# A hybrid decoder block in one program: a new priority rule for the instruction order, and one projection moved forward

## The chip, the cores and the metric

The kernel runs on one core of a Trainium2 chip. The metric is device time in microseconds, from the first to the last instruction of one launch; lower is better. The time of the kernel before is the median of 3 runs.

## The reference

Everything is float32. `x` is 512 tokens by 1024 channels. It is normalised (RMS over the channels, times a gain) and multiplied by one weight matrix `w_in` of 1024 by 6936. The product is cut into pieces that feed two mixers:

- **Mixer A**, sparse attention: 8 query heads of 64 in 2 groups. Each head attends to compressed keys (31 blocks of 32 tokens, through a small two-layer network with weights `cmp_w1`, `cmp_w2`), to selected keys (with 8 blocks and the best 16 wanted, all causal keys) and to a window of 512 (again all causal keys). Three softmaxes, each times a sigmoid gate, are summed; the sum is times silu(`z_n`), then times `w_nsa_o`, which gives `y_a`.
- **Mixer B**, retention: 4 heads, keys of 128, values of 256, in 4 chunks of 128 tokens. Each chunk adds the decayed product inside the chunk and a product with a state carried from chunk to chunk. The output is normalised per head, times silu(`z_r`), then times `w_ret_o`, which gives `y_b`.

The result is `x + rmsnorm((sigmoid(m_a) * y_a + sigmoid(m_b) * y_b) @ w_out)`. `z_n`, `z_r`, `m_a`, `m_b`, `q_r`, `k_r`, `v_r` are all columns of `h @ w_in`.

## The kernel before

**Arithmetic.** Every operand of a large product is split into a high and a low part (`whi`, `wlo` for weights, `hTh`, `hTl` for the activations), and a product is three matmuls: high by high, high by low, low by high. ScalarE (ACT) makes most of the high parts by a copy, VectorE (DVE) most of the low parts by a subtraction; GpSimd (POOL) makes some.

**Blocks.** The large projections are blocks of 512 columns. A block is 4 loads of 512 KB into a ring of 4 buffers (`raw`), 8 splits of 128 rows into a ring of 9 pairs (`whi`, `wlo`), and 4 tiles of 24 matmuls. A tile accumulates in one of two PSUM banks (`ACC`). Its tail, a coroutine, empties the bank with DVE or ACT and so frees it for the next tile but one.

**Order of the blocks.** `main()` (L1231 on) issues: the attention projections, the two products of the compression (`hidden`, L643), `z_n` (called Z here), then for each of two head pairs hp the blocks ZR (`z_r`), QK (`q_r`, `k_r`) and VR (`v_r`); then for each half of the output columns MA (`m_a`), MB (`m_b`), the product with `w_nsa_o` and that with `w_ret_o`; last `w_out`. MA0 is the first half of `m_a`, and so on. The attention of mixer A runs beside these blocks, as coroutines of their own.

**How the order of instructions is made.** Every engine works through its own instructions in the order in which the program gives them. A planner (`class Order`, L36 to L99) makes this order while the program is built: it keeps a model time `now` of TensorE (PE) and a model time at which each other engine will be free. Every piece of work is a coroutine with a fixed priority (smaller first) that yields the model time of its next input. `run()` takes the first coroutine, by priority, whose input is at least `LAG` (150 ns) old. A coroutine that has its input is issued even if its engine has much work queued before it. The splits of weights are issued as soon as the ring has room (`splitter` priority 1, `split_lo` priority 0, L358 to L391); attention has priorities 1 to 3, the blocks of `main()` 9: TensorE runs them where nothing else is ready.

**Waits that the change touches.** `tail_zr` (L920) keeps silu(`z_r`) in `zt[t]`, one set for both head pairs; so its copy for pair 1 waits until retention chunk t of pair 0 is finished (flag `ret0t`). `tail_qk` (L943) frees its bank with four DVE instructions at L198. `tail_m` (L1099) multiplies by the row of norms (`rsrow`, L185), then takes the Sigmoid on ACT; for MA0 it waits for flags of the retention or of the attention, since its buffers `sgs` lie on theirs. `ga_split` (L1116) waits until all of retention is finished, and then splits mixer A's output for the product with `w_nsa_o`, with POOL. `ret` (L980) is the retention of one chunk, in which chunk t waits for the state of chunk t - 1, and chunk 0 of pair 1 for the end of pair 0.

Of the kernel before, what the change touches and what calls it, by code (L numbers as in the profile page):

```python
# [27 lines left out]
NR, NW = 4, 9  # L28
MAIN = 9
LAG, PE_LAG = 150.0, 110.0  # L30
MARGIN = 50.0
WAKE = 10
# [3 lines left out]
class Order:  # L36
# [3 lines left out]

    def __init__(self):
        self.now = 0.0
        self.eng = {"act": 0.0, "dve": 0.0, "pool": 0.0, "dma": 0.0}
        self.ring = 500.0
        self.port = 0.0
        self.cos = []
        self.flags = set()

    def spawn(self, gen, prio):
        self.cos.append([prio, len(self.cos), 0.0, gen])  # L50
        self.cos.sort(key=lambda c: c[:2])
# [4 lines left out]
    def pe(self, cost, r=0.0):  # L56
        self.now = max(self.now, r + LAG + PE_LAG) + cost
        return self.now + 47
# [4 lines left out]
    def op(self, e, cost, r=0.0, port=False):  # L63

        self.eng[e] = self.begin(e, r, port) + cost
# [10 lines left out]
    def run(self):  # L76
        while self.cos:
            best = None
            for c in self.cos:
                w = c[2]  # L80
# [4 lines left out]
                w += LAG + (MARGIN if c[0] < MAIN else 0.0)  # L85
# [6 lines left out]
            if not callable(best[2]):  # L92
# [27 lines left out]
def block_kernel(ctx: ExitStack, tc, x, xT, g_pre, w_in, b_gate, pe_k, w1_k, w2_k,  # L120
# [51 lines left out]
    def act(o, i, func=AF.Copy, r=0.0, **kw):  # L172
        S.activation(o, i, func, **kw)  # L173
        return od.op("act", act_ns(o, i, lazy(*kw.values())), r)
# [90 lines left out]
    zt = [at(30 + 2 * t, 512) for t in range(NT)]  # L265
# [4 lines left out]
    sgs = [at(o, 512) for o in (28, 30, 8, 10, 12, 14, 16, 18)]  # L270
# [53 lines left out]
    add_block(w_in, C_Z, 512, KD, True)  # L324
    for hp in range(2):
        add_block(w_in, C_ZR + hp * 512, 512, KD)
        add_qk(hp)
        add_block(w_in, C_VR + hp * 512, 512, KD)
    for half in range(2):
        add_block(w_in, C_MA + half * 512, 512, KD)  # L330
        add_block(w_in, C_MB + half * 512, 512, KD)
        add_nsa_o(half)
        add_block(w_ret_o, half * 512, 512, KD)
# [23 lines left out]

    def splitter():  # L358
        for i, (_, n, _, perm) in enumerate(loads):
            for k in range(2):  # L360
# [3 lines left out]
                while len(raws) <= i:  # L364
                    load_next()
                r = max(raws[i][1], done[-1] if done and not own else 0.0)
                yield r
# [25 lines left out]
    used = [0]  # L393

    class Block:
# [10 lines left out]
        def ready(self, kt):  # L406
            i = self.base + kt
            return parts[i][2] + PE_LAG if i < len(parts) else (lambda: i < len(parts))
# [51 lines left out]
    def h_split():  # L460
        for k in range(KD):
            yield lambda: xTr[k] > 0
            yield xTr[k]
# [4 lines left out]
    def h_low(k, e):  # L468
        yield e
# [3 lines left out]
    def norms():  # L473

        for t in range(NT):
            yield lambda: t in xr_
            yield xr_[t]
            e = act(xt[t], xt[t], AF.Square, scale=1.0 / 32.0, accum_out=ss[:, t:t + 1], r=xr_[t])
        yield e
        e = ts(ss, ss, 1e-6, None, OP.add, r=e)  # L480
        e = tt(rs3[:, 0, :], ss, nhalf, OP.pow, e, "pool")
        yield e
# [7 lines left out]
        yield e  # L490
# [23 lines left out]
    def rope16(v, t, shape, r, e="dve"):  # L514
# [15 lines left out]
        tt(t2[hi], v[lo], bc(ropen[:, t, 24:32]), OP.mult, r, e)  # L530
        return tt(v[al], t1, t2, OP.add, 0.0, e)
# [8 lines left out]
    def keysT(kd, off, br, t, r):  # L540
# [4 lines left out]
        yield e  # L545
# [3 lines left out]
        yield e  # L549
# [4 lines left out]
    def vals(src, br, t, r):  # L554
        for g in range(2):
            sv = src[:, g * 64:(g + 1) * 64]
            e = act(VS[:, t, br, g, g, :], sv, r=r)
            e = sub_split(VS[:, t, br, g, 1 - g, :], sv, VS[:, t, br, g, g, :], e, "pool")
        return e

    def tail_a(t, ps, e, ring):
        yield od.need("const", "rs")
        kn = yield from NAT.get()
        yield max(e, constr["rope"], rsr[0])
        e = act(kn, ps, r=e, scale=rs(t))
        ring.put(ps, e)
        yield e
# [13 lines left out]
        yield ep  # L581
# [12 lines left out]
    def tail_c(t, ps, e):  # L594
        kn = yield from NAT.get()
        yield e
        e = act(kn[:, 0:280], ps[:, 0:280], r=e, scale=rs(t))
        ACC.put(ps, e)
        yield e
# [10 lines left out]
    def tail_z(j, ps, e):  # L610
        yield od.need("rsrow")
        th = yield from NAT.get()
        yield max(e, rwr[0])
        e = tt(szn[:, j, :], ps, rsrow, OP.mult, e)
        ACC.put(ps, e)
        yield e
        e = act(th, szn[:, j, :], AF.Tanh, r=e, scale=0.5)
        yield e
# [4 lines left out]
    def gates():  # L623
        yield od.need("C0", "C1", "C2", "C3")
        e = act(gate, gate, AF.Tanh, scale=0.5)
        yield e
# [3 lines left out]
    def x_split(i):  # L630
# [4 lines left out]
        yield e  # L635
# [25 lines left out]
    def compress(i, ph, e):  # L661
        yield e
# [9 lines left out]
        yield e  # L672
        pv = pt[:, 0:256].rearrange("p (k s c) -> p k s c", k=2, s=2)
        e = act(u, pv[:, :, 0, :], r=e)
        yield e
        e = tt(hx, pv[:, :, 1, :], u, OP.add, e)
        PT.put(pt, e)
        tt(u, hx, hx, OP.mult)
        ts(u, u, 0.044715, 1.0, OP.mult, OP.add)
        e = tt(u, u, hx, OP.mult)  # L680
        yield e
        e = act(u, u, AF.Tanh, scale=0.7978845608028654, r=e)
        yield e
        e = stt(hx, u, 1.0, hx, OP.add, OP.mult, e)
        po = yield from PT.get()
        if i == 0:
# [3 lines left out]
            yield e  # L690
            pv = po[:, 0:64].rearrange("p (g c) -> p g c", g=2)
            e = act(kc[:, :, 0, :], pv, scale=-0.5, r=e)
            yield e
            e = stt(kc[:, :, 1, :], pv, -0.5, f(kc[:, :, 0, :]), OP.mult, OP.subtract, e)
        else:
# [9 lines left out]
            yield e  # L705
# [11 lines left out]
    def tail_q(t, ps, e):  # L717
        qn = yield from NAT.get()
        yield e
        e = act(qn, ps, r=e, scale=rs(t, 1))  # L720
        ACC.put(ps, e)
        yield e
# [4 lines left out]
        yield e  # L727
        e = sub_split(qs[:, :, 1, :], qv, qs[:, :, 0, :], e)
        NAT.put(qn, e)
        for g in range(2):  # L730
# [5 lines left out]
            yield ep  # L736
# [17 lines left out]
    def att_cmp(t):  # L754
# [7 lines left out]
        yield e  # L762
# [6 lines left out]
        od.op("dve", 350)  # L769
        ts(mx, mx, -1.0e38, None, OP.max)  # L770
# [626 lines left out]
```

## Time and profile before

| | us |
|---|---|
| median of 3 runs (lowest to highest) | 555.47 (554.83 to 558.17) |
| the profiled execution's own time | 556.03 |
| its span in the profile | 554.2 |
| TensorE busy | 527.7 |
| VectorE busy | 385.9 |
| ScalarE busy | 257.4 |
| GpSimd busy | 69.7 |

The span is the time from the first to the last instruction in the trace. Busy times are of the whole span, and the kernel has stages with different limits. Matmuls overlap, and their ends are modelled; so the busy time of TensorE says where it had nothing to do, but not that it worked at its peak elsewhere.

### The profile page before, as it was taken

How to read it: one execution, taken by the hardware profiler on the slowest of the kernel's cores; microseconds unless marked ns; L12 is line 12 of the kernel's file. 1: busy time of each engine (PE TensorE's matmuls, PEld its weight loads, DVE VectorE, ACT ScalarE, POOL GpSimd, SP SyncE). 2: the span in 40 equal slices, each digit the busy share in tenths (PEclk: the TensorE clock that was granted, in tenths of full speed). 3: DMA queues.
4: the chain of work that ended last, by engine and by line, in shares of the span. 5: the costliest groups of instructions: out<-in, count | busy, mean ns of one | idle time of the engine just before them, and what ended most of it. 6: DMA issues, size and time to landing. Idle time of an engine off the chain costs nothing.

```text
span 554.2 us, 7494 instructions
## 1 busy us (share of the span) xinstructions
PE 527.7 (95%) x2642; PEld 441.0 (80%) x2642; DVE 385.9 (70%) x871; ACT 257.4 (46%) x550; POOL 69.7 (13%) x92
## 2 busy tenths in 40 slices
PE   8989996999999996999987999999999999999995
PEld 7778785888778785888876888887888888888885
DVE  6589899979989999877785658774545253526443
ACT  5572685647558466555371445442424143304411
POOL 1021102000100112212221233022000000000000
PEclk9989998999999999899999999999999999999998
DMA  8881037401301402305031231327422251414022
GB/s 294 290 246 41 20 97 200 160 2 38 115 0 39 135 20 84 107 2 170 1 116 56 81 109 38 115 56 247 152 77 69 84 152 30 157 43 152 1 76 114
DMA packets 34837, 55.22 MB, mean 100 GB/s; under 512 B 4336, under 2 KB 14448, under 8 KB 34800
## 3 DMA queue, kind: packets, MB, share of 16 engines
q1 hardware_dynamic: 34800, 54.75, 31.7%
q8 instruction: 20, 0.33, 0.2%
q14 instruction: 17, 0.14, 0.1%
HBM read 52.64 MB, written 2.10 MB: 99 GB/s over the span
## 4 chain that ended last, share of the span: by engine, by line
PE 68%; DVE 21%; DMA 4%; issue 3%; ACT 2%; SPq 1%; POOL 0%; DVEq 0%; POOLq 0%; ACTq 0%
PE bank L206 63%; DVE wlo L185 5%; PE bank L210 5%; DVE arena_f L194 3%; DVE arena_r L185 3%; DVE arena_f L816 3%; DVE arena_f L185 2%; DMA raw<-in_w_in_dram 2%; DMA arena_f<-in_x_dram 2%; DMA arena_f<-in_xT_dram 1%; DVE arena_f L198 1%; DVE nat L198 1%; ACT arena_f L173 1%; SPq L452 1%; ACT arena_r L173 1%
## 5 line engine op out<-in xcount | busy, mean ns | idle before, releaser
L173 ACT ACTIVATE whi<-raw 128x512 fp32r<-128x512 f32 x148 | 89.4, 626 | 60.1 <-PE bank L206 45.8
L185 DVE TENSOR_TENSOR wlo<-raw,whi 128x512 fp32r<-128x512 f32 x150 | 105.7, 745 | 7.2 <-ACT whi L173 6.5
L206 PE MATMUL bank<-whi,hTh 128*128 128x512 f32 x256 | 100.8, 409 | 6.3 <-DVE nat L198 4.8
L206 PE MATMUL bank<-wlo,hTh 128*128 128x512 f32 x256 | 96.8, 393 | 0.4 <-DVE wlo L185 0.4
L206 PE MATMUL bank<-whi,hTl 128*128 128x512 f32 x256 | 96.9, 394 | 0.0
L206 PE MATMUL bank<-arena_r 128*128 128x256 f32 (+2 forms) x328 | 73.0, 342 | 1.7 <-DVE arena_r L185 1.6
L173 ACT ACTIVATE arena_r<-bank 128x512 fp32r<-128x512 f32 (+2 forms) x80 | 45.0, 570 | 55.8 <-PE bank L210 53.3
L206 PE MATMUL bank<-hTh,whi 128*128 128x512 f32 x160 | 63.5, 397 | 0.1
L206 PE MATMUL bank<-hTh,wlo 128*128 128x512 f32 x160 | 62.6, 391 | 0.0
L206 PE MATMUL bank<-hTl,whi 128*128 128x512 f32 x160 | 62.3, 390 | 0.0
L206 PEld LDWEIGHTS bank<-whi,hTh 128*128 128x128 f32 x256 | 48.4, 189 | 14.9 <-DVE nat L198 5.3
L185 DVE TENSOR_TENSOR arena_r<-bank,arena_r 128x512 fp32r<-128x512 f32 (+2 forms) x72 | 46.6, 656 | 18.4 <-ACT arena_r L173 18.1
L206 PE MATMUL bank<-arena_r,whi 128*128 128x512 f32 x192 | 59.1, 389 | 0.0
L206 PEld LDWEIGHTS bank<-arena_r 128*128 128x128 f32 x328 | 51.1, 192 | 9.9 <-DVE arena_r L185 3.3
L206 PEld LDWEIGHTS bank<-whi,hTl 128*128 128x128 f32 x256 | 48.2, 189 | 10.8
L206 PEld LDWEIGHTS bank<-wlo,hTh 128*128 128x128 f32 x256 | 48.5, 190 | 8.7 <-DVE wlo L185 0.8
L206 PE MATMUL bank<-whi,arena_r 128*128 128x512 f32 (+1 forms) x176 | 49.0, 353 | 0.0
L210 PE MATMUL bank<-ident,arena_f 128*128 128x128 f32 (+2 forms) x262 | 40.9, 279 | 6.2 <-DVE arena_f L185 3.4
L210 PEld LDWEIGHTS bank<-ident,arena_f 128*128 128x128 f32 (+2 forms) x262 | 32.2, 142 | 17.0 <-DVE arena_f L185 5.6
L206 PEld LDWEIGHTS bank<-arena_r,whi 128*128 128x128 f32 x192 | 36.0, 188 | 7.5
L173 ACT ACTIVATE arena_f<-arena_f,stat 128x512 f32<-128x512 f32 (+3 forms) x64 | 35.3, 554 | 12.0 <-DVE stat L816 12.0
L206 PE MATMUL bank<-wlo,arena_r 128*128 128x512 f32 (+1 forms) x104 | 35.3, 349 | 4.7 <-DVE wlo L185 4.7
(118 smaller groups left out, 726.4 us busy)
## 6 DMA issues: line engine op xcount, KB each, us to landing
raw<-in_w_in_dram SPq DMA_DIRECT2D x43, 512.0 KB, 4.4
raw<-in_w_in_dram SPq DMA_DIRECT2D x18, 256.0 KB, 3.1
arena_f<-in_x_dram SPq DMA_DIRECT2D x8, 512.0 KB, 6.9
raw<-in_w_ret_o_dram SPq DMA_DIRECT2D x8, 512.0 KB, 4.7
raw<-in_w_out_dram SPq DMA_DIRECT2D x8, 512.0 KB, 5.0
arena_f<-in_xT_dram SPq DMA_DIRECT2D x8, 256.0 KB, 6.2
raw<-in_cmp_w_k_dram SPq DMA_DIRECT2D x8, 256.0 KB, 4.5
arena_f<-in_rope_r_dram SPq DMA_DIRECT2D x8, 256.0 KB, 2.6
```

Source lines behind the costliest of these rows:

```text
L173: S.activation(o, i, func, **kw)
L185: (V if e == "dve" else G).tensor_tensor(o, a, b, op=op)
L194: V.tensor_scalar(o, a, s1, s2, op0=op0, op1=op1)
L198: V.scalar_tensor_tensor(o, a, s, b, op0=op0, op1=op1)
L206: T.matmul(ps, a, b, start=start, stop=stop)
L210: T.transpose(ps, a, idn)
L452: DMA.dma_start(xTf[k], xT[k * P:(k + 1) * P, :])
L816: V.tensor_tensor_reduce(pv[:, b, :], sv[:, b, :], maskp[:, 512 - L:512], 1.0, -NEG, OP.add, OP.min, nm[:, b:b + 1])
```

## The change

`PLAN` gives the order of the blocks, in which MA0 stands between Z and the first ZR. A coroutine can now name the engine that its next instruction needs (`yield e, "dve"`); it is then held back while that engine has more than `SLACK` (700 ns) of work queued by the model. Priorities may be functions: a weight split has priority 0 if its part is at most `SOON` (2) parts ahead of what `main()` is at, and 4 otherwise. The model's costs change: 8 ns more for every operation, inputs of dependent operations on one engine counted, read-outs of accumulators counted. `either` lets the model choose DVE or POOL where POOL was fixed. `zt` has a set for each head pair: pair 1's lies on buffers of the attention, so its tail waits for the attention's end (`ATT`) and no longer for `ret0t`. `sgs[0]` to `sgs[3]` get memory of their own, `sgs[4]` to `sgs[7]` lie on pair 0's `zt`.

```diff
+PLAN = (("Z", 0), ("MA", 0), ("ZR", 0), ("QK", 0), ("VR", 0), ("ZR", 1), ("QK", 1), ("VR", 1),
+        ("MB", 0), ("NO", 0), ("RO", 0), ("MA", 1), ("MB", 1), ("NO", 1), ("RO", 1))
+SOON = 2
+ISSUE = 8.0
+SLACK = 700.0
...
     def op(self, e, cost, r=0.0, port=False):
-        self.eng[e] = self.begin(e, r, port) + cost
+        self.eng[e] = self.begin(e, r, port) + cost + ISSUE
...
-            for c in self.cos:
-                w = c[2]
+            for c in sorted(self.cos, key=lambda c: (c[0]() if callable(c[0]) else c[0], c[1])):
+                w, e = c[2] if isinstance(c[2], tuple) else (c[2], None)
...
-                w += LAG + (MARGIN if c[0] < MAIN else 0.0)
+                w += LAG + (0.0 if c[0] == MAIN else MARGIN)
+                if e:
+                    w = max(w, self.eng[e] - SLACK)
...
+    def either(n, r):
+        return "dve" if od.begin("dve", r, True) + 1.04 * n <= od.begin("pool", r, True) + 2.36 * n else "pool"
...
-    zt = [at(30 + 2 * t, 512) for t in range(NT)]
+    zt = [[at((8 if hp else 30) + 2 * t, 512) for t in range(NT)] for hp in range(2)]
-    sgs = [at(o, 512) for o in (28, 30, 8, 10, 12, 14, 16, 18)]
+    sgs = [bp.tile([P, 512], FT, name=f"sg{i}") for i in range(4)] + [at(o, 512) for o in (30, 32, 34, 36)]
...
-                od.spawn(split_lo(p, hi, lo, src, vh, vl, e), 0)
+                od.spawn(split_lo(p, hi, lo, src, vh, vl, e), rank(p))
+                nxt[0] = p + 1
...
     def split_lo(p, hi, lo, src, vh, vl, r):
+        yield lambda: rank(p)() == 0 or od.eng["dve"] <= od.now + SLACK
         yield r
-        c = size(vl)
-        e = "dve" if od.begin("dve", r, True) + 1.04 * c < od.begin("pool", r, True) + 2.36 * c else "pool"
-        r = sub_split(vl, src, vh, r, e)
+        r = sub_split(vl, src, vh, r, either(size(vl), r))
...
+    def rank(p):
+        return lambda: 0 if p <= wanted[0] + SOON else 4
...
     def tail_zr(hp, t, ps, e):
-        yield od.need("C0", "C1", "C2", "C3", "cmp0", "cmp1", *([f"ret{hp - 1}{t}"] if hp else []))
-        yield e
-        e = act(zt[t], ps, r=e, scale=rs(t, 2))
+        yield od.need("C0", "C1", "C2", "C3", "cmp0", "cmp1", *(ATT if hp else ()))
+        yield e, "act"
+        e = act(zt[hp][t], ps, r=e, scale=rs(t, 2))
...
     def tail_m(half, i, ps, e):
-        if half == 0 and i >= 2:
-            yield od.need(*(RETA if i >= 6 else ATT))
-        elif half == 0:
-            yield od.need("qk13", "ret10")
+        if half == 0 and i >= 4:
+            yield od.need(f"ret0{i - 4}")
...
-            gar[0] = sub_split(gal[:, j, :], szn[:, j, :], gah[:, j, :], e, "pool")
+            gar[0] = sub_split(gal[:, j, :], szn[:, j, :], gah[:, j, :], e, either(512, e))
...
-    od.spawn(splitter(), 1)
+    od.spawn(splitter(), lambda: rank(nxt[0])())
```

Besides these, some 60 lines of the form `yield e` become `yield e, "act"`, `"dve"` or `"pool"`.

## Rows read from the trace of the kernel before

**Rows 1.** Page, part 1: busy us, share of span, instructions.

```profile
PE 527.7 (95%) x2642; PEld 441.0 (80%) x2642; DVE 385.9 (70%) x871; ACT 257.4 (46%) x550; POOL 69.7 (13%) x92
```

**Rows 2.** Busy time by stretch: length, then engines, granted clock, DMA share, GB/s.

```profile
0.00:40.00 40.00, 35.66 (x171) 30.39 (x172) 27.02 (x66) 23.77 (x47) 6.01 (x23) 0.96 0.86 277
...
80.00:95.00 15.00, 10.32 (x73) 9.43 (x72) 14.79 (x32) 9.13 (x19) 3.98 (x3) 0.96 0.77 209
95.00:216.00 121.00, 119.02 (x626) 98.31 (x626) 111.69 (x301) 75.21 (x177) 11.24 (x10) 0.99 0.21 66
216.00:222.00 6.00, 1.25 (x7) 1.00 (x6) 6.00 (x9) 2.17 (x10) 2.33 (x3) 0.84 0.40 119
222.00:227.00 5.00, 5.00 (x17) 4.02 (x17) 4.67 (x22) 2.13 (x9) 0.67 (x1) 0.51 0.67 229
...
280.00:301.00 21.00, 16.17 (x83) 12.87 (x83) 16.70 (x37) 9.23 (x17) 5.37 (x6) 1.00 0.33 100
...
379.00:544.00 165.00, 164.90 (x734) 136.74 (x734) 73.01 (x115) 50.56 (x90) 1.32 (x3) 1.00 0.32 102
544.00:554.20 10.20, 4.42 (x37) 4.21 (x36) 4.35 (x10) 0.95 (x4) 0.86 (x2) 0.85 0.27 103
```

**Rows 3.** Timeline near 216 us: start, duration, engine, line, tiles, count [idle before].

```profile
216.61 4.16 DVE L185 TENSOR_TENSOR wlo<-raw,whi 128x512 fp32r<-128x512 f32 x5
...
220.70 0.86 DVE L198 SCALAR_TENSOR_TENSOR nat<-bank,rs,arena_f 128x256 f32<-128x256 f32 x2
...
221.62 0.80 PE L206 MATMUL bank<-whi,hTh 128*128 128x512 f32 x1 [4.75 <-DVE nat L198]
```

**Rows 4.** Waits, 280 to 301 us: us in total, times, longest.

```profile
PE bank L210 <- DVE arena_f L185: 3.4, 2, 2.7
...
PE bank L206 <- ACT arena_f L173: 1.3, 1, 1.3
```

**Rows 5.** Timeline near 297 us.

```profile
296.20 0.70 POOL L185 TENSOR_TENSOR rv<-rv,nhalf 128x2 f32<-128x2 f32 x1 [11.07 <-DVE rv L192]
...
297.84 0.87 DVE L198 SCALAR_TENSOR_TENSOR nat<-bank,rs,arena_f 128x256 f32<-128x256 f32 x2
```

**Rows 6.** Waits, 76 to 97 us.

```profile
PE bank L206 <- DVE wlo L185: 4.7, 2, 2.8
```

**Rows 7.** Groups by line and form, whole span: busy us, mean ns, idle before.

```profile
L185 DVE TENSOR_TENSOR wlo<-raw,whi 128x512 fp32r<-128x512 f32 x150 | 105.7, 745 | 7.2 <-ACT whi L173 6.5 <-PE bank L210 0.4
L185 DVE TENSOR_TENSOR arena_f<-bank,rsrow 128x512 f32<-128x512 f32 x20 | 13.7, 687 | 32.3 <-PE bank L206 32.1
L198 DVE SCALAR_TENSOR_TENSOR nat<-bank,rs,arena_f 128x256 f32<-128x256 f32 x32 | 13.7, 475 | 2.4 <-PE bank L206 2.1 <-DMA arena_f<-in_rope_r_dram 0.2
...
L173 ACT ACTIVATE arena_f<-arena_f 128x512 f32<-128x512 f32 x16 | 10.0, 628 | 30.8 <-DVE arena_f L185 30.5
```

**Rows 8.** Timeline of ACT: both table loads of the span, and what follows them.

```profile
0.72 1.28 ACT L1317 ACT_TABLE_LOAD   x1 [0.72 <-PEq L1376]
2.02 0.20 ACT L1317 ACTIVATE ss<-nhalf 128x1 f32<-128x1 f32 x1
...
350.01 1.28 ACT L173 ACT_TABLE_LOAD   x1
355.50 0.63 ACT L173 ACTIVATE arena_f<-arena_f 128x512 f32<-128x512 f32 x1 [4.21 <-DVE arena_f L185]
```

**Rows 9.** Timeline: retention's matmuls, pair 1's first chunk, weight splits, the split after retention.

```profile
278.42 2.41 PE L206 MATMUL bank<-arena_r 128*128 128x256 f32 x18
...
324.41 0.75 DVE L198 SCALAR_TENSOR_TENSOR arena_r<-bank,rs,arena_r 128x512 fp32r<-128x512 f32 x1 [2.54 <-ACT arena_r L173]
...
345.06 3.09 DVE L185 TENSOR_TENSOR wlo<-raw,whi 128x512 fp32r<-128x512 f32 x5
...
371.01 7.49 DVE L185 TENSOR_TENSOR wlo<-raw,whi 128x512 fp32r<-128x512 f32 x5
...
371.11 6.83 POOL L185 TENSOR_TENSOR arena_r<-arena_f,arena_r 128x512 fp32r<-128x512 f32 x4 [5.45 <-ACT arena_r L173]
```

More of the change, by code (lines that the diff above doesn't have):

```diff
@@ L57, in pe @@
         self.now = max(self.now, r + LAG + PE_LAG) + cost
-        return self.now + 47
+        return self.now + 75
     def begin(self, e, r=0.0, port=False):
@@ L91, in run @@
             assert best is not None, f"nothing can be issued {[c[3].__name__ for c in self.cos]} {sorted(self.flags)}"
-            if not callable(best[2]):
+            if isinstance(best[2], tuple):
+                self.now = max(self.now, best[2][0] + LAG, self.eng[best[2][1]] - SLACK)
+            elif not callable(best[2]):
                 self.now = max(self.now, best[2] + LAG)
@@ L323, in block_kernel @@
     add_w1(w1_v)
[L324 to L333, printed above, removed]
+    for name, i in PLAN:
+        if name == "Z":
+            add_block(w_in, C_Z, 512, KD, True)
+        elif name == "QK":
+            add_qk(i)
+        elif name == "NO":
+            add_nsa_o(i)
+        elif name == "RO":
+            add_block(w_ret_o, i * 512, 512, KD)
+        else:
+            add_block(w_in, {"ZR": C_ZR, "VR": C_VR, "MA": C_MA, "MB": C_MB}[name] + i * 512, 512, KD)
     for half in range(2):
@@ L364, in splitter @@
                 while len(raws) <= i:
-                    load_next()
+                    yield lambda: len(raws) > i or len(raws) < NR or len(parts) > 2 * (len(raws) - NR) + 1
+                    if len(raws) <= i:
+                        load_next()
                 r = max(raws[i][1], done[-1] if done and not own else 0.0)
-                yield r
+                yield r, "act"
                 m = n // 2
@@ L391, in split_lo @@
             load_next()
-    used = [0]
+    used, wanted = [0], [0]
+    def rank(p):
+        return lambda: 0 if p <= wanted[0] + SOON else 4
     class Block:
@@ L407, in ready @@
             i = self.base + kt
+            wanted[0] = max(wanted[0], i)
             return parts[i][2] + PE_LAG if i < len(parts) else (lambda: i < len(parts))
@@ L897, in att_sum @@
         low = yield from NAT.get()
-        yield a["e"]
+        yield a["e"], "act"
         e = act(low[m], po[o], r=a["e"])
-        yield e
+        yield e, "dve"
         e = tt(low[m], po[m], low[m], OP.add, e)
         PO.put(po, e)
-        yield e
+        yield e, "pool"
         gv = szn[m, :, t * P:(t + 1) * P]
-        e = tt(gv, low[m].rearrange("p (j c) -> p j c", j=4), gv, OP.mult, e, "pool")
+        e = tt(gv, low[m].rearrange("p (j c) -> p j c", j=4), gv, OP.mult, e, either(512, e))
         NAT.put(low, e)
@@ L997, in ret @@
             ek = act(knh, kf[t])
-            yield ek
-            ek = sub_split(knl, kf[t], knh, ek, "pool")
+            yield ek, "pool"
+            ek = sub_split(knl, kf[t], knh, ek, either(256, ek))
         pa = yield from PS.get()
@@ L1265, in main @@
             yield from hidden(i)
-        blk = Block(8, 512)
-        for j in range(4):
-            ps, e = yield from tra(blk, j, j == 3, *hT_of)
-            od.spawn(tail_z(j, ps, e), 1)
-        for hp in range(2):
+        for name, i in PLAN:
+            if name in ("NO", "RO"):
+                blk = Block(4 if name == "NO" else 8, 512)
+                xh, xl = (gah, gal) if name == "NO" else (gbh, gbl)
+                if name == "NO":
+                    yield od.need("ga")
+                yield (gar if name == "NO" else gbr)[0] + PE_LAG
+                for ft in range(4):
+                    ps, e = yield from tra(blk, ft, ft == 3, lambda kt: xh[:, kt, :], lambda kt: xl[:, kt, :])
+                    od.spawn((tail_ya if name == "NO" else tail_yb)(i, ft, ps, e), 1)
+                continue
@@ L1271, in main @@
             blk = Block(8, 512)
             for t in range(NT):
-                ps, e = yield from nat(blk, t, 512, t == NT - 1)
-                od.spawn(tail_zr(hp, t, ps, e), 1)
-            blk = Block(8, 512)
-            for t in range(NT):
-                ps, e = yield from nat(blk, t, 512, t == NT - 1)
-                od.spawn(tail_qk(hp, t, ps, e), 1)
-            blk = Block(8, 512)
-            for t in range(NT):
-                ps, e = yield from nat(blk, t, 512, t == NT - 1)
-                od.spawn(ret(hp, t, ps, e), 1)
@@ L1283, in main @@
-        od.spawn(ga_split(), 1)
-        for half in range(2):
-            for i in range(2):
-                blk = Block(8, 512)
-                for ft in range(4):
-                    ps, e = yield from tra(blk, ft, ft == 3, *hT_of)
-                    od.spawn(tail_m(half, i * 4 + ft, ps, e), 1)
-            blk = Block(4, 512)
-            yield od.need("ga")
-            yield gar[0] + PE_LAG
-            for ft in range(4):
-                ps, e = yield from tra(blk, ft, ft == 3, lambda kt: gah[:, kt, :], lambda kt: gal[:, kt, :])
-                od.spawn(tail_ya(half, ft, ps, e), 1)
-            blk = Block(8, 512)
-            yield gbr[0] + PE_LAG
-            for ft in range(4):
-                ps, e = yield from tra(blk, ft, ft == 3, lambda kt: gbh[:, kt, :], lambda kt: gbl[:, kt, :])
-                od.spawn(tail_yb(half, ft, ps, e), 1)
+                if name in ("Z", "MA", "MB"):
+                    ps, e = yield from tra(blk, t, t == 3, *hT_of)
+                    od.spawn(tail_z(t, ps, e) if name == "Z" else tail_m(i, t + 4 * (name == "MB"), ps, e), 1)
+                else:
+                    ps, e = yield from nat(blk, t, 512, t == NT - 1)
+                    od.spawn({"ZR": tail_zr, "QK": tail_qk, "VR": ret}[name](i, t, ps, e), 1)
@@ L1302, in merged @@
+            if (name, i) == ("VR", 1):
+                od.spawn(ga_split(), 1)
         def merged(kt):
```

201 lines of the change are left out of this document (102 added, 99 removed).

## The prediction

> **What bounds the kernel now.** I read the page's busy times first, then the busy time by stretch, then for each stretch with a gap the timeline and the waits, and last the groups of instructions for durations. TensorE (PE) is busy for 527.7 of 554.2 us [rows 1], so 26.5 us are the most that any order could win by filling gaps. The stretches say where they are [rows 2]: 4.3 us in the first 40 us, 4.7 in 80 to 95, 2.0 in all of 95 to 216, 4.75 in 216 to 222, 4.8 in 280 to 301, and 5.8 in the last 10.2; 227 to 280 and 301 to 544 have next to none. The start and the end are not touched by the change.
>
> The reader is to see two things more in these rows. From 95 to 216 us, where attention runs, PE is busy for 119.0 of 121 us and VectorE (DVE) for 111.7: both are nearly full, and there is no hole of 21 us in which a block more would be free. And from 379 us on PE does 734 matmuls in 164.9 us, 0.225 us each, while DVE is busy for 73 us of 165: this end stage is PE's alone.
>
> The gap at 216 is a queue. Five low parts of weights hold DVE for 4.16 us; behind them in its queue stand the L198 instructions that free a bank of QK0, and PE waits 4.75 us for them [rows 3]. Then the granted clock is 0.51 from 222 to 227 us, the lower of its two levels (1.2 instead of 2.4 GHz), right after PE stood idle; PE's 5.0 busy us there hold work for half as long, so 2.5 us more are lost [rows 2].
>
> The gap at 280 to 301 is the waits of 3.4 and 1.3 us [rows 4]. The bank of a ZR1 tile can't be emptied before retention chunk t of pair 0 has left `zt[t]`; and in DVE's queue the freeing of a QK1 bank at 297.84 stood behind an instruction that waited for POOL's power at 296.20 [rows 5].
>
> **The change, part by part.**
>
> *MA0 moved.* 96 matmuls of 0.225 us leave the PE-bound end stage, 21.6 us, and come back in front of ZR0. Since PE is full there as well, this sums to nothing by itself: as much of QK0 and VR0 slides behind the attention's end. It changes what fills which gap. MA0's own load on DVE is 8 low parts of 0.745 and 4 products of 0.687 us, 8.7 us; the QK0 that slides out has 8 of 0.745, 16 of 0.475 and 4 low parts of its transposes of 0.69 (taken like the 0.687), 16.3 us [rows 7]. The attention stage, where DVE is 92% busy, gets 7.6 us lighter. MA0's 4 loads go through the queue of SP, ahead of ZR0's; the DMA engines are 21% busy in that stage [rows 2], so I cost them at nothing, and they are covered as long as the four `raw` buffers stay a block ahead.
>
> *Priorities for splits, and no issue into a long queue.* At 216 us a bank's release (priority 1) would now go ahead of low parts that are more than two parts early (priority 4). Gain between 0 (the same parts are wanted just then) and 4.75 + 2.5 = 7.2 us. I take 7.2, since these five parts were for later tiles, and the tiles in their place then, MA0's and ZR0's, free a bank with one instruction instead of four.
>
> *`zt` for each pair.* ZR1 waits for the attention's end alone, and has that behind it. Gain between 0 and 4.8 us; I take 4.8. What is late next is `qk1t`, which still waits for `ret0t`; but ZR1, 21.6 us of PE work, now stands as cover in between.
>
> *The Sigmoids among the Exps.* This is the cost. The trace has two table loads on ACT: one at the start, and one of 1.28 us at 350.01 before the first Sigmoid at 355.50; between them Exp, Tanh, Square and copies run without one [rows 8]. So a Sigmoid needs a table that the Exps don't use. MA0's four Sigmoids now fall into the time of the Exps, a tile apart. At best the trace's one load merely comes earlier (if the Sigmoid's table serves Exp too, which no row shows): 0. At worst there is one load to and one back for each: 8 of 1.28 = 10.3 us, which the planner doesn't know of. I take 8 loads. What of them reaches the end? ACT is busy for 75.2 of 121 us [rows 2], so 38% fall into its idle time; of the other 6.4 us I let half through, 3.2, because DVE, which waits for ACT's results, has just become 7.6 us lighter. The range keeps 0 and 10.3.
>
> The Trainium skill ("ScalarE: Activation LUTs", "Table sets: the hidden batching unit") speaks against this step: it lists exp with tanh in one set and sigmoid with tanh in another, and tells to do all calls of one set before the next. The trace agrees so far that one load lasts for 348 us of Exp and Tanh. By its section "What ACT_TABLE_LOAD costs" a switch is 1283 ns plus a drain of 1380, 2.66 us in all; the 1283 is this trace's load, the drain is not to be seen: after the first load ACT goes on at 2.02 us, 0.02 us after its end [rows 8]. By that figure eight switches would be 21.3 us.
>
> *Less cover behind the retention.* The product with `w_nsa_o` waits until all of retention and `ga_split` are done. From pair 1's first chunk at 324.41 to the start of `ga_split` at 371.11 are 46.7 us; then POOL takes 6.83 [rows 9]. Before, MA0 and MB0 lay in between; now MB0 alone. PE's work from that point is 72 matmuls of VR1 (16.2 us), MB0 (21.6), and the retention's own: 68 of 256 columns at 2.41/18 = 0.134 and some 16 transposes at 0.15, 11.5 us; 49.3 together. `ga_split` is now free to go to DVE: 4 low parts of 0.69 and one ACT copy of 0.63 ahead, 3.4 us, so 50.1 us against 49.3: PE waits 0.8 us. With POOL it would be 4.2; nothing, if the chain is shorter without the five low parts in its way at 345.06 [rows 9]. I take 0.8.
>
> *DVE or POOL by `either`.* Where POOL works beside it, DVE slows: five low parts take 7.49 us beside `ga_split`, and 3.09 at 345 us [rows 9]. Moving work to DVE wins up to 4.4 us of such slowing there and costs DVE up to 0.69 us for each; that stage is PE-bound, so 0.
>
> *The rest.* The gap at 80 to 95 us is PE waiting for low parts of the compression's weights [rows 6], with DVE busy for 14.8 of 15 us [rows 2]; the order of the blocks is the same there. A better order could win the 4.7; splits that start later, only two parts ahead, could lose as much again. I take 0.
>
> **The sum**, against the execution's own 556.0 us: - 7.2 - 4.8 + 3.2 + 0.8 = 548.0. That execution lies 0.6 above the median, so I forecast 547.4 us, 1.5% faster. 1%, about what a measurement of this kernel can tell from no change, is 549.9 and 561.0.
>
> **The rivals.**
>
> *The table switches decide, and the kernel is slower.* A gate holds ACT for 1.28 + 0.63 + 1.28 = 3.2 us in one piece. ACT feeds DVE and so PE, all in fixed order; the row at 216 us shows that 4 us of one engine's queue is enough to stop PE and that its clock then falls. If each of the four does this, 12.8 us are lost, and the gain at 216 is eaten by these new stalls: 556.0 - 4.8 + 12.8 = 564.0, so 563 by the median. It decides from the point where the four holds cost more than the 12.0 us won. For it: the planner has no such cost, and nothing but attention's work stands ready then. Against: ACT is idle for 38% of that time, and PE has MA0's and ZR0's matmuls, which need no ACT until their tile is full. The Trainium skill's figure with the drain would give 556 - 12 + 21.3 = 565, on the same side.
>
> *No room: the gaps move.* With PE 98% and DVE 92% busy, a stall taken away at 216 comes back a few us later, since DVE has the same low parts to make anyway. Only `zt` pays: 556.0 - 4.8 + 3.2 = 554.4, so 554. For it: the new rule puts off low parts, it removes none. Against: the 7.6 us by which DVE gets lighter.
>
> *All gaps close.* The new rule fills 80 to 95 as well, and 95 to 216, and the loads hide: 556.0 - 4.7 - 2.0 - 4.75 - 2.5 - 4.8 = 537.2, so 537. Against: the waits for the first low parts after a load, which no priority mends.
>
> **How the numbers follow.** Chances: forecast 0.47 (its own range 543 to 552), all gaps 0.12, no room 0.23, table switches 0.18. Faster by over 1%: all gaps, and most of the forecast, 0.40, together 0.52. Within 1%: the rest of the forecast and nearly all of "no room", 0.28. Slower: the switches and a little more, 0.20. The range 538 to 562 leaves out the best of the one and the worst of the other, 2 in 10.
>
> **What would show it.** In the changed trace: no PE wait for DVE L198 of over 2 us near 200 to 230 and the clock at 1.00 there; no wait between VR0 and QK1 of over 1 us; ten table loads, eight between about 150 and 200 us; PE's gap before the first `w_nsa_o` matmul under 2 us; the end stage about 143 us instead of 165. The forecast is wrong if PE's idle time in the attention stage grows by more than the 12 us won (then the switches, seen as waits of DVE for ACT right after each load), or if the sum of PE's idle time stays at 26.5.

## The result: 3.5% faster, past the fast end of the range

The changed kernel takes 537.02 us (median of 4 runs, 536.61 to 537.67), the kernel before 556.64 beside it (4 runs, 554.83 to 558.17). The ratio is 0.965, with a 95% interval of 0.961 to 0.969. The forecast was 547.4, the range ended at 538. The profiled execution took 536.74 us by its own time; its span is 534.8, from the first to the last instruction in the trace.

Page, part 1, of the kernel after (busy us, share of span, instructions; answers to [rows 1]):

```profile
PE 521.1 (97%) x2642; PEld 437.2 (82%) x2642; DVE 387.9 (73%) x911; ACT 265.2 (50%) x560; POOL 36.5 (7%) x50
```

The reader is to subtract here. PE's idle time is 534.8 - 521.1 = 13.7 us, against 26.5 before: 12.8 us less. Its busy time fell by 6.6 us with the same 2642 matmuls. Together that is the whole 19.4 us by which the span is shorter.

Busy time by stretch of the kernel after (length, then PE, PEld, DVE, ACT, POOL, granted clock, DMA share, GB/s; answers to [rows 2]):

```profile
0.00:40.00 40.00, 36.01 (x189) 30.78 (x190) 27.41 (x79) 24.50 (x52) 4.37 (x18) 1.00 0.81 275
80.00:95.00 15.00, 13.30 (x86) 11.11 (x86) 13.58 (x28) 13.33 (x30) 1.29 (x1) 1.00 0.79 236
95.00:216.00 121.00, 119.37 (x615) 99.33 (x615) 107.81 (x278) 80.64 (x175) 8.44 (x6) 1.00 0.23 67
216.00:222.00 6.00, 6.00 (x33) 5.04 (x32) 5.52 (x16) 1.56 (x3) 0.00 (x0) 1.00 0.15 44
222.00:227.00 5.00, 5.00 (x30) 4.31 (x29) 4.78 (x18) 2.76 (x9) 0.00 (x0) 1.00 0.20 52
280.00:301.00 21.00, 21.00 (x114) 18.06 (x113) 16.19 (x36) 9.82 (x19) 3.33 (x3) 1.00 0.25 71
379.00:524.60 145.60, 145.60 (x650) 120.81 (x649) 66.66 (x106) 41.78 (x75) 1.34 (x3) 1.00 0.33 103
524.60:534.80 10.20, 4.40 (x37) 4.20 (x35) 4.33 (x10) 0.95 (x4) 0.84 (x2) 0.93 0.27 103
```

Of the 12.8 us of idle time 4.75 are those of 216 to 222, 4.8 those of 280 to 301, and 3.0 those of 80 to 95. The busy time fell with the clock: in [rows 2] it is 0.51 from 222 to 227 and below 1.00 in five stretches more, here only in the last; over the span its mean rose from 0.985 to 0.999.

What PE still waits for over the span, the largest first (us in total, times, longest; answers to [rows 4] and [rows 6]):

```profile
PE bank L220 <- DVE arena_f L560: 2.6, 2, 2.2
PE bank L1331 <- POOL nhalf L241: 1.4, 1, 1.4
PE bank L216 <- DVE wlo L195: 1.0, 1, 1.0
PE bank L220 <- DVE arena_f L204: 1.0, 1, 1.0
PE bank L220 <- ACT arena_f L183: 0.4, 1, 0.4
...
```

From 205 to 301 us there is none. The largest, 2.6 at L560, was 2.5 before (L536 there); 2.2 us of it fall between 20 and 40 us, long before the attention.

### The profile page after: what moved, and what is told of

Same layout as the page of the kernel before. It is cut to its first block, busy times and chain, and to the rows that moved or that the text cites. A ratio compares the mean times of both kernels' runs of the same rounds, so it can differ in the third digit from the quotient of the medians.

```text
span 534.8 us, 7434 instructions
## 1 busy us (share of the span) xinstructions
PE 521.1 (97%) x2642; PEld 437.2 (82%) x2642; DVE 387.9 (73%) x911; ACT 265.2 (50%) x560; POOL 36.5 (7%) x50
## 4 chain that ended last, share of the span: by engine, by line
PE 78%; DVE 10%; DMA 5%; ACT 3%; issue 2%; SPq 1%; POOL 0%; POOLq 0%; DVEq 0%; ACTq 0%
PE bank L216 73%; PE bank L220 5%; DVE arena_f L195 3%; DVE wlo L195 2%; DMA arena_f<-in_x_dram 2%; DVE arena_r L195 1%; DMA arena_f<-in_xT_dram 1%; DMA raw<-in_w_in_dram 1%; ACT arena_f L183 1%; ACT L183 1%; ACT arena_r L183 1%; DMA raw<-in_cmp_w_v_dram 1%; DVE arena_f L204 1%; DVE arena_f L208 1%; DVE arena_f L840 1%
## 5 line engine op out<-in xcount | busy, mean ns | idle before, releaser
L195 DVE TENSOR_TENSOR wlo<-raw,whi 128x512 fp32r<-128x512 f32 x145 | 96.3, 699 | 12.3 <-ACT whi L183 10.4
L216 PE MATMUL bank<-whi,hTh 128*128 128x512 f32 x256 | 99.6, 404 | 0.1
L216 PE MATMUL bank<-arena_r 128*128 128x256 f32 (+2 forms) x328 | 70.3, 335 | 0.6 <-DVE stat L840 0.4
L220 PE MATMUL bank<-ident,arena_f 128*128 128x128 f32 (+2 forms) x262 | 39.4, 274 | 4.6 <-DVE arena_f L560 2.6
L220 PEld LDWEIGHTS bank<-ident,arena_f 128*128 128x128 f32 (+2 forms) x262 | 31.2, 139 | 13.6 <-DVE arena_f L560 3.3
L216 PE MATMUL bank<-arena_r,wlo 128*128 128x512 f32 x96 | 37.3, 389 | 0.0
```

The lines of the kernel that those rows point to most:

```text
L195: (V if e == "dve" else G).tensor_tensor(o, a, b, op=op)
L216: T.matmul(ps, a, b, start=start, stop=stop)
L220: T.transpose(ps, a, idn)
```

## The experiments

All times are medians of 4 or 5 runs; each ratio is to the kernel before on the same chip, with its 95% interval. Differences are taken between medians, some of them from different chips; the kernel before took 556.4 to 557.1 us beside them. "Whole" is the changed kernel, whose second measurement is here:

> The changed kernel itself, unaltered, so that the next three are compared with it on the same chip: 536 to 538 us.

It took 536.76 us, 0.9651 (0.9628 to 0.9675).

### The change part by part

**The gate buffers alone, on the kernel before.**

```diff
-    zt = [at(30 + 2 * t, 512) for t in range(NT)]
+    zt = [[at((8 if hp else 30) + 2 * t, 512) for t in range(NT)] for hp in range(2)]
...
-        yield od.need("C0", "C1", "C2", "C3", "cmp0", "cmp1", *([f"ret{hp - 1}{t}"] if hp else []))
+        yield od.need("C0", "C1", "C2", "C3", "cmp0", "cmp1", *(ATT if hp else ()))
...
```

The merge gates `sgs` get the memory of the whole here too, and `tail_m` its waits, since the old `sgs` lay on the same buffers.

> The kernel before with the gate buffers of the two pairs apart (and the memory of the merge gates that goes with it), nothing else. My term: the waits of 280 to 301 us go, 4.8 us: 551 to 553 us. If the gap only moves into the next wait, 555 to 557 us. With the run of the old rule and the new block order (546.0 us) the difference is MA0's place alone: 5 to 7 us by theory 'filler', which says that the old rule too had little left to do at 216 to 254 us.

550.47 us, 0.9884 (0.9861 to 0.9906): 5.9 us less than before, a little past the 551 to 553 expected. The stall at 216 us is still there, whole (PE's waits from 205 to 235 us):

```profile
PE bank L206 <- DVE nat L198: 4.8, 1, 4.8
```

**The wait for the gate buffers put back into the whole.**

```diff
-        yield od.need(..., *(ATT if hp else ()))
+        yield od.need(..., *((*ATT, f"ret0{t}") if hp else ()))
```

> The changed kernel, in which a ZR1 tile again waits for retention chunk t of pair 0 before its bank is emptied; memory stays apart. By my term it loses 4.8 us: 541 to 543 us. If MA0's place has put enough other work beside that chunk, it loses nothing: 536 to 538 us.

542.6 us, 0.9756 (0.972 to 0.9792): 5.6 to 5.8 us more than the whole. The waits between 280 and 310 us are back, in about the size of [rows 4]:

```profile
PE bank L216 <- ACT arena_f L183: 2.4, 2, 1.6
PE bank L220 <- DVE arena_f L195: 1.6, 1, 1.6
```

Both directions agree, and both are about 1 us above the 4.8 of the forecast.

**MA0's new place too, still with the old rule.** To the gate buffers comes MA0 between Z and ZR0; costs, priorities and POOL's work stay as before.

```diff
+        blk = Block(8, 512)
+        for ft in range(4):
+            ps, e = yield from tra(blk, ft, ft == 3, *hT_of)
+            od.spawn(tail_m(0, ft, ps, e), 1)
...
```

> The kernel before, with its planner as it was, but MA0 behind Z and the gate buffers of the two pairs apart. Theory 'rule': the stall of several us in the attention stage and that at 80 to 95 us stay, those of 280 to 301 us go: 548 to 553 us; the eight table loads that this planner does not know of add up to 3 us. Rival 'place': 537 to 543 us.

546.0 us, 0.9813 (0.9785 to 0.9841), between the two expected ranges: 4.5 us less than the gate buffers alone, intervals apart. From 205 to 235 us PE now waits for nothing. So MA0's place is enough to remove the stall of [rows 3], under the old priorities: the forecast had given it to the new ones.

**The whole with MA0 behind VR1 again.**

```diff
-PLAN = (("Z", 0), ("MA", 0), ("ZR", 0), ("QK", 0), ("VR", 0), ("ZR", 1), ("QK", 1), ("VR", 1),
+PLAN = (("Z", 0), ("ZR", 0), ("QK", 0), ("VR", 0), ("ZR", 1), ("QK", 1), ("VR", 1), ("MA", 0),
```

> The changed kernel with its blocks in the order of the kernel before: MA0 stands behind VR1 again; everything else of the change stays. Theory 'rule' (the new rule for issuing took the waits of TensorE away, wherever MA0 stands): 537 to 541 us, with TensorE idle for about 14 us of its span and no wait of over 2 us between 95 and 300 us. Rival 'place' (MA0 in the attention stage made VectorE lighter by 7.6 us and so removed the gaps): 545 to 551 us, with waits of TensorE back near 200 to 230 us. If the table loads cost anything, this one, which has 2 loads and not 10, wins up to 3 us back.

550.61 us, 0.9908 (0.9878 to 0.9937): 13.6 us more than the whole. All the rest of the change is worth only some 6 us without MA0's move, as much as the gate buffers alone.

And yet the stall at 216 us is gone here too, at a clock of 1.00 (columns as in the result's busy times):

```profile
216.00:222.00 6.00, 6.00 (x31) 4.93 (x31) 5.68 (x16) 1.67 (x4) 0.00 (x0) 1.00 0.00 0
222.00:227.00 5.00, 5.00 (x28) 4.19 (x26) 4.22 (x18) 4.01 (x12) 1.30 (x1) 1.00 0.34 106
```

So the new rule, with its costs and free choice, removes that stall as well; without MA0's move nothing is won by it, since a larger hole opens behind 229 us (below).

**DVE or POOL, and the model's costs.** First the free choice on top of MA0's place, with the old costs:

```diff
+    def either(n, r):
+        return "dve" if od.begin("dve", r, True) + 1.04 * n <= od.begin("pool", r, True) + 2.36 * n else "pool"
...
-        e = tt(gv, low[m].rearrange("p (j c) -> p j c", j=4), gv, OP.mult, e, "pool")
+        e = tt(gv, low[m].rearrange("p (j c) -> p j c", j=4), gv, OP.mult, e, either(512, e))
...
```

> The kernel before with MA0 behind Z and the gate buffers apart (546.0 us), and the five kinds of operations free to go to VectorE or GpSimd, by the old model's costs. With the new costs as well it was 541.0 us. If the free choice is the source of those 5 us, 540 to 542.5 us; if the new costs are, 544.5 to 547 us.

543.62 us, 0.9767 (0.9744 to 0.979), 2.4 less, between the two expected ranges. Then the whole without the **guard** (that nothing is issued to an engine with more than `SLACK` queued) and without the splits' changing priority, so with the free choice and the new costs:

```diff
-SLACK = 700.0
+SLACK = 1.0e9
...
-        return lambda: 0 if p <= wanted[0] + SOON else 4
+        return lambda: 0
...
-    od.spawn(splitter(), lambda: rank(nxt[0])())
+    od.spawn(splitter(), 1)
```

> The changed kernel without the two parts of the new rule: no coroutine is held back for a long queue (SLACK without limit), and weight splits have fixed priorities 1 and 0 as before. The new model costs, MA0's place and the gate buffers stay. Theory 'rule': 546 to 552 us, a queue of low parts in front of a bank's release is back, and the granted clock falls below 0.9 in a slice. Rival 'place' or 'model costs': 537 to 541 us.

540.96 us, 0.973 (0.9704 to 0.9757), 2.6 less again; this step takes in whatever else of the planner changed, such as which of two coroutines of equal priority goes first. Each of these two steps has an interval that touches its neighbour's; both together, 5.0 us, are clear. The 4.0 us from here to the whole are what guard and priority add.

The other way, the five kinds of work fixed on POOL again in the whole:

```diff
-            e = sub_split(VS[:, t, br, g, 1 - g, :], sv, VS[:, t, br, g, g, :], e, either(64, e))
+            e = sub_split(VS[:, t, br, g, 1 - g, :], sv, VS[:, t, br, g, g, :], e, "pool")
...
-            gar[0] = sub_split(gal[:, j, :], szn[:, j, :], gah[:, j, :], e, either(512, e))
+            gar[0] = sub_split(gal[:, j, :], szn[:, j, :], gah[:, j, :], e, "pool")
```

> The changed kernel, in which the five kinds of operations that were fixed on GpSimd are fixed there again (value splits, mixer A's gate product, the rotation's additions, the keys' and the last split); only weight splits choose. I cost this part at nothing: 536 to 538 us. Rival: VectorE runs slower beside GpSimd (low parts of weights took 745 ns on average before, 699 after), and the last split holds TensorE up for about 4 us before the first product with w_nsa_o: 540 to 544 us.

547.63 us, 0.9837 (0.981 to 0.9864): 10.7 more than the whole, and above both expected ranges. And only the last of the five, `ga_split`, with the last two lines of this diff alone:

> The changed kernel with ga_split alone fixed on GpSimd again; with all five kinds fixed it was 547.6 us. My step 'less cover': TensorE then waits 4.2 us instead of 0.8 before the first product with w_nsa_o, and low parts of weights run slower beside GpSimd at that time: 538 to 541 us. If all of the 10.9 us come from this one split, 546 to 549 us; if the four kinds in the attention stage and the retention are what counts, 536.5 to 538.5 us.

537.63 us, 0.9658 (0.9642 to 0.9674), within the intervals of the whole; PE waits 0.7 us for that split. So most of the 10.7 is not in `ga_split`. With all five fixed PE is idle for 3.1 us from 216 to 301 us, at a mean clock of 0.96, where the whole has no idle time and 1.00; that is the attention's end (below). Another 1.8 us are waits for `ga_split` behind the retention. The rest is not traced to one place.

**The splits' priority fixed, the guard kept.**

```diff
-        return lambda: 0 if p <= wanted[0] + SOON else 4
+        return lambda: 0
...
-    od.spawn(splitter(), lambda: rank(nxt[0])())
+    od.spawn(splitter(), 1)
```

> The changed kernel with fixed priorities of the weight splits (1 and 0), while coroutines are still held back for a long queue. Without both parts of the rule it was 541.0 us. If the splits' priority is what counts, 540 to 542 us, with low parts of 80 to 95 us late again; if holding back is what counts, 536.5 to 538 us.

550.39 us, 0.9892 (0.9861 to 0.9923): 13.4 more than the whole, 9.4 more than with neither, and above both expected ranges. The two edits don't add up: without the priority the guard costs 9.4 us, and the two together win 4.0. The priority without the guard was not run, so whether the guard adds anything to it is open.

### Why MA0's place is worth so much

Beside the attention, TensorE has only what doesn't wait for it: Z, MA0 if it stands there, ZR0, QK0 and VR0's tiles up to the two banks that VR0's tails hold until the attention's last parts are done (`ret`'s first line). This work is its **filler**. If it runs out early, PE is left to the attention's own chain of dependent steps.

One view shows this: busy time by stretch of only those instructions that read `hTh`, which is two in three of the matmuls of the filler and none of the attention's (columns: PE, PEld, DVE, ACT, clock, DMA share, GB/s). The stretch 229 to 253.5 us, first of the whole:

```profile
229.00:253.50 24.50, 15.93 (x50) 8.74 (x50) 0.00 (x0) 0.00 (x0) 1.00 0.37 108
```

of the kernel before:

```profile
229.00:253.50 24.50, 14.72 (x47) 8.24 (x47) 0.00 (x0) 0.00 (x0) 1.00 0.04 12
```

and of the whole with MA0 behind VR1:

```profile
229.00:253.50 24.50, 0.28 (x2) 0.00 (x0) 0.00 (x0) 0.00 (x0) 0.78 0.27 76
```

With MA0 behind VR1 the new rule gets through the filler by 229 us, and then has 24.4 us without a matmul of it (229.12 to 253.54). What ends this is a release of VR0's banks, right behind the attention's last product with a gate (251.56; that kernel's DVE):

```profile
251.56 0.69 DVE L195 TENSOR_TENSOR arena_f<-nat,arena_f 64x512 f32<-64x512 f32 x1
252.28 0.43 DVE L195 TENSOR_TENSOR arena_r<-arena_f,arena_r 128x256 fp32r<-128x256 f32 x1
252.73 1.41 DVE L208 SCALAR_TENSOR_TENSOR arena_r<-bank,rs,arena_r 128x512 fp32r<-128x512 f32 x2
```

PE is idle for 8.5 us there, at a lower clock (all instructions of that kernel):

```profile
216.00:240.00 24.00, 21.56 (x108) 17.33 (x108) 21.77 (x76) 15.22 (x44) 6.74 (x5) 0.93 0.26 76
240.00:280.00 40.00, 33.91 (x170) 27.90 (x169) 26.85 (x70) 18.79 (x47) 2.69 (x3) 0.87 0.05 15
```

Over the span that kernel has PE idle for 18.7 us, against 13.7 in the whole, and busy for 528.0 us, against 521.1, with the same 2642 matmuls: more of the loss is slow clock (0.984 on the mean, against 0.999) than idle time.

Against this stood a rival: MA0 helps because it makes DVE's work lighter there, by the 7.6 us of the forecast. The experiment that tells them apart leaves MA0 behind VR1 and gives VR0's first two tiles buffers of their own, so that they no longer wait for the attention: more filler, and no less work for DVE (158.4 busy us from 95 to 275, against 156.5 with MA0 behind VR1 alone). The merge gates of half 0 move to the buffers of `zt` for it and wait for the retention.

```diff
-    VR = [Ring([(at(o, 512, FR), at(o + 2, 512, FR)) for o in os]) for os in ((12, 8), ())]
+    sgt = [bp.tile([P, 512], FR, name=f"vr{i}") for i in range(4)]
+    VR = [Ring([(sgt[0], sgt[1]), (sgt[2], sgt[3])] + [(at(o, 512, FR), at(o + 2, 512, FR)) for o in (12, 8)]), Ring([])]
...
-        yield od.need(*[f"att{i}{g}" for i in (2, 3) for g in range(2)])
+        if hp or t >= 2:
+            yield od.need(*[f"att{i}{g}" for i in (2, 3) for g in range(2)])
...
```

> The changed kernel with MA0 behind VR1, as in the run with the old block order (550.6 us), but with buffers of their own for the first two tiles of VR0, so that these two no longer wait for attention and the next two find buffers as soon as two of its four quarters are done; MA0 and MB0 get their buffers from both pairs' zt. Theory 'filler' (in the old order the blocks that don't wait for attention run out at about 216 us, and TensorE has only attention's own matmuls until 252): two to four tiles of 5.4 us more to do in that hole, 540 to 546 us, and the hole starts later. Theory 'light' (MA0 wins because it asks less of VectorE than the block it displaces): VR0's tails ask as much of VectorE as MA0 or more and nothing is displaced, 549 to 552 us.

543.64 us, 0.9766 (0.9737 to 0.9795): 7.0 us less than with MA0 behind VR1 alone, half of what MA0's place gives. The stretch has filler again:

```profile
229.00:253.50 24.50, 10.72 (x34) 5.54 (x33) 0.00 (x0) 0.00 (x0) 1.00 0.22 65
```

The hole is now from 247.3 to 258.4, 11.2 us instead of 24.4.

The traces speak against the rival too. Busy time from 95 to 275 us, first with MA0 behind VR1, then in the whole, and the whole's last product with a gate:

```profile
95.00:275.00 180.00, 171.47 (x877) 143.10 (x877) 156.50 (x425) 100.87 (x246) 16.19 (x15) 0.96 0.20 63
```

```profile
95.00:275.00 180.00, 178.37 (x921) 149.00 (x921) 161.06 (x422) 115.74 (x263) 14.83 (x12) 1.00 0.26 76
```

```profile
262.74 0.69 DVE L195 TENSOR_TENSOR arena_f<-nat,arena_f 64x512 f32<-64x512 f32 x1
```

DVE (the third number behind the length) does 4.6 us more there with MA0 in front, not less, and the attention reaches that product 11 us later, at 262.74 instead of 251.56. So MA0 doesn't win by a shorter attention: PE has filler up to its end. For the new rule the cause is the filler. Under the old rule, where the move gave 4.5 us, DVE is 3.1 us lighter from 95 to 216 (108.5 against 111.7), and no run separates the two.

The two kernels with a large loss above have the same hole late: with the priority fixed from 261.2 to 274.6 us, where the last product with a gate starts at 272.6, and with POOL fixed from 265.5 to 270.4, where it starts at 269.0. PE's longest wait from 250 to 290 us, first with the priority fixed, then with POOL fixed:

```profile
PE bank L216 <- DVE arena_r L208: 3.0, 1, 3.0
...
```

```profile
PE bank L216 <- DVE arena_r L208: 3.1, 1, 3.1
```

Both are VR0's release again. Busy time near there, with the priority fixed:

```profile
261.00:275.00 14.00, 6.38 (x21) 3.90 (x20) 10.39 (x24) 5.73 (x13) 0.00 (x0) 0.74 0.48 152
```

and with POOL fixed:

```profile
260.00:275.00 15.00, 11.88 (x49) 9.53 (x49) 11.91 (x22) 7.72 (x14) 4.27 (x4) 0.82 0.54 158
```

The whole has PE busy for 15.00 of 15.00 us in 260 to 275, at a clock of 1.00. Why the attention ends 6 to 10 us later in these two is not settled: each edit moves dozens of instructions.

### The table loads

The gates as Tanh, which needs no other table than the one in use (its trace has one load, at the start, instead of ten): sigmoid(x) is (1 + tanh(x/2)) / 2, with the half put into the split of the sum.

```diff
-        e = act(sgs[i], sgs[i], AF.Sigmoid, r=e)
+        e = act(sgs[i], sgs[i], AF.Tanh, r=e, scale=0.5)
...
-        e = tt(sgs[ft], sgs[ft], ps, OP.mult, e)
+        e = stt(sgs[ft], sgs[ft], 1.0, ps, OP.add, OP.mult, e)
...
```

> The changed kernel with every merge gate computed by Tanh of half its argument instead of Sigmoid; the one added and the factor one half go into instructions that are there already (VectorE's multiplication becomes a scalar_tensor_tensor). So there is one table load instead of ten, nothing else changes in number. If the eight loads among the Exps cost what I forecast (3.2 us), 533 to 534.5 us; if ScalarE's idle time hides them, 536 to 537.5 us, no difference; if they cost their whole 10.3 us, 526 to 528 us.

535.0 us, 0.962 (0.9595 to 0.9645). Measured again beside the whole:

> The changed kernel with gates by Tanh once more, beside the changed kernel. If the eight table loads cost about 2 us, as the first look says, the difference is 1.5 to 2.5 us; if ScalarE's idle time hides them and the first look was chance, under 0.7 us.

535.93 us, 0.9633 (0.9608 to 0.9658). So the eight loads among the Exps, and a ninth in the end stage, cost 0.8 to 2.0 us by the two measurements; the intervals overlap with the whole's. It is the fastest version run, by little.

Then more loads: a Sigmoid of one column, whose result nothing reads, ahead of each Tanh of Z and of ZR.

```diff
+    junk = cp.tile([P, 1], FT, name="junk")
...
+        act(junk, nhalf[:, 0:1], AF.Sigmoid)
```

> The changed kernel with one Sigmoid of 128 by 1 put ahead of each Tanh of the Z and ZR tails, its result unused. Each that falls among the Exps brings a table load to and one back: 8 for Z, up to 8 for ZR of pair 0, about 2 more later. If a load costs what the eight of the change do (2 us in 8, 0.25 each), 540 to 542 us. If the loads are hidden only while they are few, and ScalarE's queue then stops TensorE (my rival of the switches), over 548 us.

547.17 us, 0.9842 (0.981 to 0.9874), between the two expected ranges, with 24 loads instead of 10: 10.4 us for 14 loads, 0.74 each, in which 12 added Sigmoids of 0.20 us are counted too. In 95 to 216 us ACT goes from 80.64 busy us to 94.95, and PE from 119.37 to 115.08:

```profile
95.00:216.00 121.00, 115.08 (x581) 92.05 (x579) 99.60 (x259) 94.95 (x183) 7.72 (x6) 1.00 0.18 54
```

DVE's waits for ACT grow in that stretch, most of all this one, which was 0.7 in the whole:

```profile
DVE arena_f L208 <- ACT nat L183: 5.0, 5, 1.9
```

PE's waits there, all of them for DVE, are 4.8 us against 1.6. So the mechanism of the first rival, ACT holding up DVE and so PE, exists; eight loads aren't enough for it.

## Why the prediction was wrong

The forecast took 8.0 us off the execution's own 556.0; 19.4 us of span went. Set against the steps as they were measured, one on top of the other (the loads' and the cover's price lies in MA0's step):

| step | forecast | measured |
|---|---|---|
| `zt` apart | -4.8 | -5.9 |
| MA0 moved, table loads, less cover | 0 + 3.2 + 0.8 | -4.5 |
| `either` | 0 | -2.4 |
| the model's costs ("The rest") | 0 | -2.6 |
| splits' priority and guard | -7.2 | -4.0 |

**The step that failed** is "MA0 moved": "Since PE is full there as well, this sums to nothing by itself". It gave 4.5 us under the old rule (5.3 to 6.5 by an estimate that adds the loads' 0.8 to 2.0 back) and 13.6 under the new one. I had counted work, which is indeed the same, and taken a stretch that is busy on the mean for one that is full all the way. What counts in that stretch is whether PE has filler up to the attention's end. MA0's 21.6 us of matmuls are more of it. Under the old rule they took the place of the QK0 tiles that stalled at 216; the new rule uses filler up faster, and without MA0 has none left at 229 us.

**The stall at 216.** Its 4.75 and 2.5 us did go, but the 7.2 are not the priority's. MA0's place alone removes the stall under the old rule. The new rule alone removes it too, but there the time is lost again behind 229 us. Priority and guard are worth 4.0 us on top of all the rest.

**80 to 95 us.** I took 0 for the gap behind the low parts, under "The rest"; 3.0 of its 4.7 us went. PE's busy time in that stretch, with MA0's place alone, then with the free choice added, then with the rule but POOL fixed:

```profile
80.00:95.00 15.00, 10.23 (x70) 9.31 (x68) 14.79 (x31) 8.19 (x18) 3.98 (x3) 0.93 0.74 193
```

```profile
80.00:95.00 15.00, 13.36 (x82) 11.90 (x81) 14.86 (x34) 10.66 (x23) 1.85 (x1) 0.89 0.75 218
```

```profile
80.00:95.00 15.00, 14.33 (x90) 11.73 (x90) 13.83 (x27) 11.75 (x25) 0.00 (x0) 1.00 0.97 279
```

Either edit closes most of it by itself, and in both POOL does less there (1.85 and 0.00 busy us against 3.98). For `either`, "that stage is PE-bound, so 0" was wrong: it reaches stages where DVE sets the pace.

**The clock.** I priced one fall of it, 2.5 us. PE's busy time fell by 6.6, since the clock stays up in the other stretches as well. A gap that closes can give back its length and a slow stretch behind it. It need not: from 280 to 301 us PE was idle for 4.8 us before, and the clock was 1.00 there [rows 2].

**The table loads.** Eight between 131 and 169 us, two for each gate, as forecast, though 150 to 200 us was expected; the cost of 3.2 was too high: 0.8 to 2.0. ACT's timeline of the whole (start, duration, operation):

```profile
142.64 1.28 ACT L183 ACT_TABLE_LOAD   x1
143.93 0.63 ACT L183 ACTIVATE sg<-sg 128x512 f32<-128x512 f32 x1
144.58 1.28 ACT L183 ACT_TABLE_LOAD   x1
145.88 0.72 ACT L183 ACTIVATE arena_f<-arena_f,stat 128x512 f32<-128x512 f32 x1
```

A gate holds ACT for 3.24 us from 142.64 to 145.88, the 3.2 of the rival. The Trainium skill ("ScalarE: Activation LUTs", "What ACT_TABLE_LOAD costs") adds a drain of 1380 ns to each switch; the trace doesn't agree, since the next instruction starts 1.29 and 1.30 us after each load began, 0.01 to 0.02 us after its end, and the second load begins 0.02 us after the Sigmoid's end. The Trainium skill's rule to batch calls by set (same page, "Table sets: the hidden batching unit") would keep the Sigmoids out of the Exps' time. That is worth 0.8 to 2.0 us here, less than MA0's place gives.

**Right as forecast:** `zt`; no wait of note between VR0 and QK1; the end stage, 145.6 us instead of 164.9 (about 143 expected); no PE wait ahead of the product with `w_nsa_o`, where 0.8 us was taken.

**The rivals.** "All gaps close" gave 537.2 by the execution's own time, and it came to 536.74. I gave it 0.12. Its sum was right by terms that partly weren't: 80 to 216 us gave 3.3 rather than 6.7, the clock 6.6 rather than 2.5. Its "against", that no priority mends the waits for low parts, didn't hold. "No room" fails for the whole on the 13.7 us of idle time left. Without MA0's move it describes what happened: the stall at 216 goes, a hole comes a few us later, and only `zt`'s part of the gain is left (550.6 us); but the hole is a lack of filler, not the low parts that the rival named. The table switches fail on the Tanh version.

## What to carry to other kernels

Where a chain of dependent steps runs beside independent blocks on the bottleneck engine, ask up to when these blocks last, not how busy the engine is on the mean; moving one more such block ahead of the chain's end can pay for the holes that it fills and for the slow clock behind them. Price edits to a static order together: MA0's move gave 4.5 or 13.6 us, and the guard lost 9.4 without the priority that goes with it. When a gap of TensorE closes, look at the granted clock behind it: a slow stretch there belongs to the gain.

## What the runs showed of the hardware

- A table load is 1.28 us of ACT, but what reaches the end was less: 0.8 to 2.0 us in all for the eight among the Exps and a ninth, and 0.74 us each for 14 more. ACT is busy for 80.64 and 94.95 of the 121 us there. That its idle time hides the rest is the likely reason, not a measured one.
- Beside POOL a low part on DVE takes longer: five took 7.49 us beside POOL's `ga_split` [rows 9]. In the whole that split is on DVE, and there each takes 0.68 to 0.69 us; the mean over the span fell from 745 ns [rows 7], while POOL went from 69.7 to 36.5 busy us:

```profile
372.60 0.69 DVE L195 TENSOR_TENSOR arena_r<-bank,arena_r 128x512 fp32r<-128x512 f32 x1
373.20 0.68 DVE L195 TENSOR_TENSOR wlo<-raw,whi 128x512 fp32r<-128x512 f32 x1
373.80 0.69 DVE L195 TENSOR_TENSOR arena_r<-arena_f,arena_r 128x512 fp32r<-128x512 f32 x1
374.40 0.69 DVE L195 TENSOR_TENSOR wlo<-raw,whi 128x512 fp32r<-128x512 f32 x1
```

```profile
L195 DVE TENSOR_TENSOR wlo<-raw,whi 128x512 fp32r<-128x512 f32 x145 | 96.3, 699 | 12.3 <-ACT whi L183 10.4
```

With the five kinds of work fixed on POOL again, and POOL busy for 69.8 us, the mean goes back up:

```profile
L195 DVE TENSOR_TENSOR wlo<-raw,whi 128x512 fp32r<-128x512 f32 x152 | 105.4, 731 | 9.1 <-ACT whi L183 7.7 <-PE bank L216 1.0
```
